# RWKV in a hybrid trunk: the inverse joined to blocks of 64 on TensorE, transitions and states kept per head

## The chip, the cores and the metric

The kernel runs on one core of one Trainium2 chip. The metric is the device time of one execution in microseconds, the median of several runs. Matrix products run on TensorE (PE, with its weight loads as PEld), element-wise work on VectorE (DVE), ScalarE (ACT) and GpSimd (POOL); SyncE (SP) issues most DMAs. Each engine takes its instructions strictly in order.

## What is computed

A two-layer trunk over 512 tokens (256 context, 256 latent) of width 1024. Each layer has four token mixers, and one of them is a bidirectional RWKV-7 with 8 heads of 64. Its recurrence, run once forward and once backward, is all that the change touches:

```python
def _rwkv7_scan(s0, seq, d, reverse):
    def step(s, inp):
        r_t, w_t, k_t, v_t, kk_t, a_t = inp
        s = (s * w_t[:, :, None, :]
             - jnp.einsum('bhvk,bhk->bhv', s, kk_t)[..., None] * (kk_t * a_t)[:, :, None, :]
             + v_t[..., None] * k_t[:, :, None, :])
        return s, jnp.einsum('bhvk,bhk->bhv', s, r_t)
    s_fin, o = lax.scan(step, s0, xs, reverse=reverse)
```

The state `s` is 64x64 per head. Context starts from zero, latent tokens start from the state that the context leaves. In layer 1 only the latent outputs are wanted.

## The kernel before

The sequence is cut into 8 chunks of 64 tokens, and the scan into products of matrices within a chunk and a short recurrence from chunk to chunk. `rwkv()` runs over four pairs of heads `i` (two heads share the 128 partitions) and in each over two directions `d`. For a pair the phases are, in the order of the code: projections of the pair (`pre`, L543 to L568), the decay and the chunk matrices of each direction (`f0`, `f1`, L580 to L697), the inverse (`inv`, L698 to L762), then the projections of the *next* pair, then `b0` (L774 to L822), `b1` (L824 to L862) and the group norm (`fin`, L864 to L882).

**Inverse.** Each chunk has a unit triangular system of 64. `inv` inverts its two diagonal blocks of 32, in `Wt` (drawn as `Wz`): blocks of 16 by substitution on DVE (L730, L732), transposed twice (L739, L740), then joined to 32 by two bursts of 64 products of 16x16x16 (L749 and the like; drawn as `Pr,U` and `Pr,Ai`), and written to `Wt` by ACT (L760) and DVE (L761). The coupling between the two blocks of 32 is not in `Wt`: POOL copies it to `U2` (L721).

**b0** applies the inverse to `B_` per direction and half `q`: four products with `Wt` into a bank, ACT copies the bank to `y1` (L788), 8 products with `U2` (L793, drawn `y,U`), copies to `y2` (DVE L794, ACT L795), 8 more products with the lower block of `Wt` into the first bank (L799, drawn `y,Wz`), and then the copies `Ev` (L801) and `fv` (L804, L805). Then per direction the transitions `GT` of the chunks: identity plus 16 products (L818, drawn `bkt,Ev`), a pair of heads at once as [128, 128], with the products between different heads masked away by a DVE multiplication with `bd` (L821).

**b1** is the recurrence: seven steps `n`, both directions in turn. A step is one product `bkt`·`fv` of 128x128x128, from the second step on one `GT`·`Z` of the same size, and a DVE scaling that writes the next `Z` (L837). The state `Z` is [128, 8, 128], of which only the two diagonal blocks are read. Then come the readouts (drawn `sr,Ev`, `sr,fv`, `re,Z`).

**What sets the order.** All products go through the helper `mm` at L352, so that the profile gives them one line; they are told apart by their operands. Between the phases stand calls of `fill`: they hand out the products of the gate projection (drawn `hh,wh`, `hl,wh`, `hh,wl`, of 512 columns in layer 0 and 256 in layer 1), work that nothing in RWKV waits for and that keeps PE busy. They are called fillers here. A scheduler orders the instructions of each engine from the code, its dependencies and its own costs, so the diff does not show where fillers end up. PSUM has eight banks: 0 and 1 for projections and fillers, 2 and 3 for `inv`, 4 to 6 for `b0`, `b1` and the norm, 7 for the output. One f32 product shows as two records on PE.

Of the kernel before, what the change touches and what calls it, by code (L numbers as in the profile page):

```python
# [9 lines left out]
F32 = mybir.dt.float32  # L10
# [3 lines left out]
AF = mybir.ActivationFunctionType  # L14
OP = mybir.AluOpType
# [279 lines left out]
class Trunk:  # L295
# [210 lines left out]
    def rwkv(self, l, dst, yo):  # L506
        nc, A, tc = self.nc, self.A, self.tc
        last = l == NL - 1
# [8 lines left out]
        with ExitStack() as es:  # L517
# [53 lines left out]
            for i in range(4):  # L571
# [145 lines left out]
                V_.scalar_tensor_tensor(A16, Ai[:, :, 0:16], lo16, Ai[:, :, 16:32], op0=OP.mult, op1=OP.add)  # L717

                U2 = R.tile([128, 2, 8, 32], F32, name="U2")
                for o in (0, 64):  # L720
                    G_.tensor_copy(U2[o:o + 32], U[o:o + 32, :, :, o // 64, 32:64])  # L721
                X2 = Xt[:, 0:512].rearrange("p (t e s) -> p t e s", t=16, e=2)
# [34 lines left out]
                for q in range(4):  # L757
                    sl = slice(32 * q, 32 * q + 32)
                    wt = Wt[sl, :, sl].rearrange("p z (e t) -> p e t z", e=2)
                    nc.scalar.activation(wt[:, 0], xt[sl, :, 0, :], AF.Copy, scale=lo16[sl])  # L760
                    V_.scalar_tensor_tensor(wt[:, 1], xt[sl, :, 1, :], hi16[sl], p2v[sl].rearrange("p z t -> p t z"),  # L761
                                            op0=OP.mult, op1=OP.add)  # L762
                while self.early:
                    self.fill(1)
# [10 lines left out]
                for d in range(2):  # L775
# [4 lines left out]
                    for q in range(2):  # L780
                        py = self.ps("bx")
                        pv = py.rearrange("p (s c) -> p s c", s=4)
                        for s in range(4):
                            self.mm(pv[:, s, :], Wt[:, 8 * d + 4 * q + s, :], B_[:, 4 * q + s, :], start=(s == 0),
                                    stop=False)
                        y12 = R.tile([128, 2, 4, 128], F32, name="y12", tag=("S0" if q == 0 else "S1") if last else "Ai" if q == 0 else "Xi")
                        y1, y2 = y12[:, 0], y12[:, 1]
                        nc.scalar.activation(y1, pv, AF.Copy)  # L788
                        p2 = self.ps("bx")
                        p2v = p2.rearrange("p (s c) -> p s c", s=4)  # L790
                        for s in range(4):
                            for o in (0, 64):
                                self.mm(p2v[o + 32:o + 64, s, :], U2[o:o + 32, d, 4 * q + s, :], y1[o:o + 32, s, :])  # L793
                        V_.tensor_copy(y2[32:64], p2v[32:64])  # L794
                        nc.scalar.activation(y2[96:128], p2v[96:128], AF.Copy)  # L795
                        for s in range(4):
                            for o in (32, 96):
                                sl = slice(o, o + 32)
                                self.mm(pv[sl, s, :], Wt[sl, 8 * d + 4 * q + s, sl], y2[sl, s, :], start=False,  # L799
                                        stop=(s == 3))  # L800
                        nc.scalar.activation(Ev[:, 2 * q:2 * q + 2].rearrange("p c h k -> p (c h) k"),  # L801
# [5 lines left out]
                for d in range(2):  # L807
# [7 lines left out]
                    for c2 in range(4):  # L815
                        for par in range(2):
                            o = 64 * par
                            self.mm(pts[par][:, c2 * 128:c2 * 128 + 128], Ev[o:o + 64, c2],  # L818
                                    bkt[o:o + 64, 2 * c2 + par, :], start=False)
                    for par in range(2):  # L820
                        V_.tensor_mul(GT[:, par:8:2, :], pts[par].rearrange("p (c k) -> p c k", c=4),  # L821
                                      bd[:, None, :].to_broadcast([128, 4, 128]))  # L822
                self.fill(FQ[l][i][3])
                self.phase(f"rw{l}.{i}.b1")  # L824
                orders = ((0, 1, 2, 3, 4, 5, 6, 7), (3, 2, 1, 0, 7, 6, 5, 4))
                for d in range(2):
                    Z = R.tile([128, 8, 128], F32, name="Z", tag="Z" if d else "Z0" if last else "Xi")
                    G_.memset(Z[:, orders[d][0], :], 0.0)
                    ZZ.append(Z)
                for n in range(7):  # L830
                    for d in range(2):
                        Z, c, cn = ZZ[d], orders[d][n], orders[d][n + 1]
                        pz = self.ps("bx")
                        self.mm(pz[:, 0:128], BKT[d][:, c, :], FV[d][:, c], start=True, stop=(n == 0))
                        if n:
                            self.mm(pz[:, 0:128], GG[d][:, c, :], Z[:, c, :], start=False)
                        V_.tensor_scalar(Z[:, cn, :], pz[:, 0:128], PT[d][:, c:c + 1], None, op0=OP.mult)  # L837
                for d in range(2):
# [19 lines left out]
                    for c in range(q0, 8):  # L858
                        for h in range(2):
                            hs = slice(64 * h, 64 * h + 64)  # L860
                            self.mm(po[hs, 64 * c:64 * c + 64], Z[hs, c, hs], re[hs, c - q0, :], start=False,
                                    stop=(d == 1 and c == 7))  # L862
# [1147 lines left out]
```

## Time and profile before

| | us |
|---|---|
| median of 3 runs | 3611.53 (3610.74 to 3620.73) |
| the profiled execution | 3617.56, its span 3615.6 |
| RWKV of layer 0, four pairs | about 160 to 640 of the span |
| RWKV of layer 1, four pairs | about 1716 to 2090 of the span |

Most of the rest of the span (other mixers, the expert layers from about 2580 on) doesn't share code with the change. The mean granted clock of TensorE over the span was 0.942 of full speed; its two levels are 1.2 and 2.4 GHz.

How to read the rows further down: a row of a timeline gives the start in us, the duration in us (of a group of xN instructions, from the first start to the last end), engine, line, operation, `out<-in`, tile and shape, and in brackets the idle time just before with what ended it. Records of PE overlap, so the price of a group is the distance from its start to the next start, not its duration.

### The profile page before, as it was taken

Reading aid. Unit: us, or ns where it says so; the run is one execution under the profiler, and the core shown is the slowest. Engines: PE = TensorE matmul, PEld = TensorE weight load, DVE = VectorE, ACT = ScalarE, POOL = GpSimd, SP = SyncE. Lnnn points to the kernel's source line nnn. Section 1 sums busy time; section 2 is a strip of 40 time slices with the busy share of each in tenths; the row PEclk is TensorE's granted clock in tenths of the full one; section 3 lists DMA queues with packets and bytes.
Section 4 is the critical chain, followed back from the end, with each engine's and each line's share of the span. In section 5 each row is a group of like instructions: output and inputs, shape, how many; then the busy total and the mean of one; then the engine's idle time right before and its main releaser. Section 6 shows DMA issues by size and latency. Waiting matters only on the chain. (4 is left out here: it accounts for less than half of the span.)

```text
span 3615.6 us, 53416 instructions
## 1 busy us (share of the span) xinstructions
PE 3303.8 (91%) x20522; PEld 2560.1 (71%) x20522; DVE 2305.2 (64%) x3375; ACT 1688.3 (47%) x2509; POOL 943.0 (26%) x873
## 2 busy tenths in 40 slices
PE   7999999998878999998988898877899999999998
PEld 3477677776656677776776687666787877877776
DVE  3555653257985423226565536885799889888887
ACT  3333433332333322234443444343677677777675
POOL 2222322134444344444322333544100000000000
PEclk9999999998989999998998899877899999999999
DMA  7511112322115255532111243114599899899895
GB/s 234 163 58 51 59 53 83 112 70 74 54 34 188 83 151 167 158 107 76 57 54 46 67 130 103 51 52 158 220 354 348 341 356 339 323 361 360 332 354 220
DMA packets 195895, 596.82 MB, mean 165 GB/s; under 512 B 22440, under 2 KB 48490, under 8 KB 152112
## 3 DMA queue, kind: packets, MB, share of 16 engines
q1 hardware_dynamic: 177824, 564.15, 44.4%
q10 hardware_dynamic: 17808, 29.18, 2.4%
q8 instruction: 163, 2.67, 0.3%
q14 instruction: 100, 0.82, 0.1%
HBM read 576.53 MB, written 16.71 MB: 164 GB/s over the span
## 5 line engine op out<-in xcount | busy, mean ns | idle before, releaser
L378 DVE TENSOR_TENSOR mwl<-mw,mwh 128x1024 fp32r<-128x1024 f32 x672 | 796.2, 1227 | 43.0 <-ACT mwh L375 41.9
L378 POOL TENSOR_TENSOR wl<-w,wh 128x512 fp32r<-128x512 f32 (+1 forms) x436 | 576.2, 1327 | 914.7 <-ACT wh L375 775.7
L375 ACT ACTIVATE wh<-w 128x512 fp32r<-128x512 f32 x536 | 333.5, 626 | 823.7 <-PE bank L352 580.5
L375 ACT ACTIVATE mwh<-mw 128x1024 fp32r<-128x1024 f32 x672 | 674.9, 1054 | 77.5 <-PE bank L352 73.5
L352 PE MATMUL bank<-mwh,mX 128*128 128x512 f32 x1792 | 570.9, 396 | 0.0
L352 PE MATMUL bank<-hh,wh 128*128 128x512 f32 (+1 forms) x1152 | 438.5, 382 | 31.6 <-ACT hh L481 5.1
L352 PE MATMUL bank<-hh,wl 128*128 128x512 f32 (+1 forms) x1152 | 433.4, 377 | 21.9 <-DVE wl L378 11.6
L352 PE MATMUL bank<-hl,wh 128*128 128x512 f32 (+1 forms) x1152 | 431.0, 374 | 1.8 <-DVE hl L482 1.7
L352 PEld LDWEIGHTS bank<-mwh,mX 128*128 128x128 f32 x1792 | 336.8, 188 | 76.2
L352 PE MATMUL bank<-mwl,mX 128*128 128x512 f32 x896 | 366.7, 409 | 2.2
L352 PEld LDWEIGHTS bank<-hh,wh 128*128 128x128 f32 x1152 | 232.4, 202 | 86.1 <-issue 30.9
L352 PE MATMUL bank<-mwh,mgT 128*128 128x512 f32 x896 | 283.4, 395 | 0.0
L352 PEld LDWEIGHTS bank<-hh,wl 128*128 128x128 f32 x1152 | 231.8, 201 | 65.1 <-DVE wl L378 14.1
L352 PEld LDWEIGHTS bank<-hl,wh 128*128 128x128 f32 x1152 | 232.8, 202 | 48.5 <-issue 16.1
L352 PEld LDWEIGHTS bank<-mwl,mX 128*128 128x128 f32 x896 | 168.4, 188 | 56.5 <-DVE mwl L378 20.9
L352 PEld LDWEIGHTS bank<-mwh,mgT 128*128 128x128 f32 x896 | 168.2, 188 | 40.4
L352 PE MATMUL bank<-mwl,mgT 128*128 128x512 f32 x448 | 178.4, 398 | 0.4
L1724 POOL TENSOR_SCALAR mPg<-moec,rtq,rtG 128x128 f32<-128x128 f32 x16 | 20.9, 1315 | 573.7 <-PE bank L1726 549.7
L378 DVE TENSOR_TENSOR wl<-w,wh 128x512 fp32r<-128x512 f32 x100 | 83.2, 837 | 99.7 <-ACT wh L375 95.3
L352 PE MATMUL bank<-fhh,wl 128*128 128x512 f32 x352 | 137.6, 392 | 1.7 <-POOL wl L378 1.7
L352 PE MATMUL bank<-fhh,wh 128*128 128x512 f32 x352 | 138.7, 397 | 0.0
L352 PE MATMUL bank<-fhl,wh 128*128 128x512 f32 x352 | 137.7, 391 | 0.9 <-DVE fhl L482 0.9
(569 smaller groups left out, 5816.8 us busy)
## 6 DMA issues: line engine op xcount, KB each, us to landing
mw<-in_moe_dram SPq DMA_DIRECT2D x336, 1024.0 KB, 6.3
w<-in_win_dram SPq DMA_DIRECT2D x304, 256.0 KB, 2.8
adaw<-in_ada_dram SPq DMA_DIRECT2D x192, 256.0 KB, 3.8
w<-in_ffn_dram SPq DMA_DIRECT2D x128, 256.0 KB, 3.0
w<-in_wbr_dram SPq DMA_DIRECT2D x64, 256.0 KB, 2.9
gdram<-gth ACTq DMA_DIRECT2D x32, 256.0 KB, 2.0
bth<-gdram SPq DMA_DIRECT2D x32, 256.0 KB, 3.5
w<-in_wout_dram SPq DMA_DIRECT2D x32, 256.0 KB, 5.4
```

Of the source, the lines that this page charges most:

```text
L352: return self.nc.tensor.matmul(out, lhsT, rhs, start=start, stop=stop, skip_group_check=True)
L375: nc.scalar.activation(xh, x, AF.Copy)
L378: (nc.gpsimd if lo == "p" else nc.vector).tensor_tensor(xl, x, xh.bitcast(F32), op=OP.subtract)
L1724: nc.gpsimd.tensor_scalar(Pg, slots[:, 0:CAP], qq[:, t, e:e + 1], G[:, t, e:e + 1], op0=OP.is_equal, op1=OP.mult)
```

## The change

The inverse is completed to blocks of 64 in `inv`: the upper-left inverse is transposed (two DVE transposes), 32 products of 32x32x32 with `U` give T2 (drawn `Pr,U` 32x32), ACT and DVE copy it out of the bank, 32 more products with the lower-right inverse (drawn `Wz,Ai` 32x32) give the missing block, and ACT and DVE copy it into `Wt`. With it `b0` needs a single product per chunk and head; `U2`, `y12`, their 16 products per half and their copies go. `GT` is made of 32 products of 64x64x64 per direction pair in place of 16 of 64x128x128, so that nothing is to be masked, and is copied out by DVE and ACT. The state `Z` shrinks to [128, 8, 64], and each product of the recurrence is split into one per head. `Z` of the first direction has a buffer of its own in both layers.

```diff
-                U2 = R.tile([128, 2, 8, 32], F32, name="U2")
-                for o in (0, 64):
-                    G_.tensor_copy(U2[o:o + 32], U[o:o + 32, :, :, o // 64, 32:64])
...
+                p1, p2 = self.mx_ps(), self.mx_ps()
+                p1v, p2v = [x.rearrange("p (z t) -> p z t", z=16) for x in (p1, p2)]
+                Wn = Pt_[:, 0:512].rearrange("p (z t) -> p z t", z=16)
+                T2 = At[:, 512:1024].rearrange("p (z t) -> p z t", z=16)
+                for o in (0, 64):
+                    sl = slice(o, o + 32)
+                    V_.transpose(Wn[sl], Wt[sl, :, sl])
+                for z in range(16):
+                    for o in (0, 64):
+                        self.mm(p1v[o + 32:o + 64, z], U[o:o + 32, z // 8, z % 8, o // 64, 32:64], Wn[o:o + 32, z])
+                nc.scalar.activation(T2[32:64], p1v[32:64], AF.Copy)
+                V_.tensor_copy(T2[96:128], p1v[96:128])
+                for z in range(16):
+                    for o in (0, 64):
+                        hi = slice(o + 32, o + 64)
+                        self.mm(p2v[o:o + 32, z], T2[hi, z], Wt[hi, z, hi])
+                nc.scalar.activation(Wt[0:32, :, 32:64], p2v[0:32], AF.Copy)
+                V_.tensor_copy(Wt[64:96, :, 96:128], p2v[64:96])
...
-                            self.mm(pv[:, s, :], Wt[:, 8 * d + 4 * q + s, :], B_[:, 4 * q + s, :], start=(s == 0),
-                                    stop=False)
-                        y12 = R.tile([128, 2, 4, 128], F32, name="y12", tag=("S0" if q == 0 else "S1") if last else "Ai" if q == 0 else "Xi")
-                        y1, y2 = y12[:, 0], y12[:, 1]
-                        nc.scalar.activation(y1, pv, AF.Copy)
-                        p2 = self.ps("bx")
-                        p2v = p2.rearrange("p (s c) -> p s c", s=4)
-                        for s in range(4):
-                            for o in (0, 64):
-                                self.mm(p2v[o + 32:o + 64, s, :], U2[o:o + 32, d, 4 * q + s, :], y1[o:o + 32, s, :])
-                        V_.tensor_copy(y2[32:64], p2v[32:64])
-                        nc.scalar.activation(y2[96:128], p2v[96:128], AF.Copy)
-                        for s in range(4):
-                            for o in (32, 96):
-                                sl = slice(o, o + 32)
-                                self.mm(pv[sl, s, :], Wt[sl, 8 * d + 4 * q + s, sl], y2[sl, s, :], start=False,
-                                        stop=(s == 3))
+                            self.mm(pv[:, s, :], Wt[:, 8 * d + 4 * q + s, :], B_[:, 4 * q + s, :])
...
-                        for par in range(2):
-                            o = 64 * par
-                            self.mm(pts[par][:, c2 * 128:c2 * 128 + 128], Ev[o:o + 64, c2],
-                                    bkt[o:o + 64, 2 * c2 + par, :], start=False)
-                    for par in range(2):
-                        V_.tensor_mul(GT[:, par:8:2, :], pts[par].rearrange("p (c k) -> p c k", c=4),
-                                      bd[:, None, :].to_broadcast([128, 4, 128]))
+                        for h in range(2):
+                            hs = slice(64 * h, 64 * h + 64)
+                            for par in range(2):
+                                o = 64 * par
+                                self.mm(pts[par][hs, c2 * 128 + 64 * h:c2 * 128 + 64 * h + 64], Ev[o:o + 64, c2, h],
+                                        bkt[o:o + 64, 2 * c2 + par, hs], start=False)
+                    V_.tensor_copy(GT[:, 0:8:2, :], pts[0].rearrange("p (c k) -> p c k", c=4))
+                    nc.scalar.activation(GT[:, 1:8:2, :], pts[1].rearrange("p (c k) -> p c k", c=4), AF.Copy)
...
-                        self.mm(pz[:, 0:128], BKT[d][:, c, :], FV[d][:, c], start=True, stop=(n == 0))
+                        for h in range(2):
+                            hs = slice(64 * h, 64 * h + 64)
+                            self.mm(pz[hs, 0:64], BKT[d][:, c, hs], FV[d][:, c, h], start=True, stop=(n == 0))
                         if n:
-                            self.mm(pz[:, 0:128], GG[d][:, c, :], Z[:, c, :], start=False)
-                        V_.tensor_scalar(Z[:, cn, :], pz[:, 0:128], PT[d][:, c:c + 1], None, op0=OP.mult)
+                            for h in range(2):
+                                hs = slice(64 * h, 64 * h + 64)
+                                self.mm(pz[hs, 0:64], GG[d][hs, c, hs], Z[hs, c, :], start=False)
+                        V_.tensor_scalar(Z[:, cn, :], pz[:, 0:64], PT[d][:, c:c + 1], None, op0=OP.mult)
```

Where the scheduler puts this on PE is seen at three places. The number after a bank or tile only tells allocations apart.

First, PE in layer 0, pair 1, where the inverse ends and `b0` begins. Before, the products with `Wt` follow on fillers and on the column norm `t,rwc` of the next pair's projections, with the first `y,U` of a half behind four fillers:

```order
751 L352 MATMUL bank2_2615<-t0_2613,rwc_354 128x512
752 L352 MATMUL bank5_2624<-B__2014,Wz_530 128x128 x4
753 L352 MATMUL bank4_2653<-B__2014,Wz_530 128x128 x4
754 L352 MATMUL bank1_2771<-hh_265,wh_2774 128x512
755 L352 MATMUL bank1_2771<-hl_266,wh_2774 128x512
756 L352 MATMUL bank1_2771<-hh_265,wl_2775 128x512
757 L352 MATMUL bank1_2771<-hh_265,wh_2774 128x512
758 L352 MATMUL bank6_2631<-y12_2629,U2_2228 32x128 x8
```

Now the join stands ahead of `t,rwc`, in four pieces among fillers, behind twelve fillers that follow `Pr,Ai`:

```order
732 L352 MATMUL bank0_2669<-hh_265,wh_2672 128x512
733 L352 MATMUL bank2_2432<-Pr_2249,U_1993 32x32
734 L352 MATMUL bank0_2669<-hl_266,wh_2672 128x512
735 L352 MATMUL bank0_2669<-hh_265,wl_2673 128x512
736 L352 MATMUL bank0_2669<-hh_265,wh_2672 128x512
737 L352 MATMUL bank2_2432<-Pr_2249,U_1993 32x32 x31
738 L352 MATMUL bank0_2669<-hl_266,wh_2672 128x512
739 L352 MATMUL bank0_2669<-hh_265,wl_2673 128x512
740 L352 MATMUL bank0_2669<-hh_265,wh_2672 128x512
741 L352 MATMUL bank0_2669<-hl_266,wh_2672 128x512
742 L352 MATMUL bank3_2433<-Wz_530,Ai_2247 32x32
```

Fillers that stood between the pieces of `y` now stand between the pieces of the join; twelve more follow before `t,rwc`, and sixteen between the third and the fourth group of `B_,Wz`.

Second, PE in the recurrence of layer 0, pair 0. Before, single products of the two kinds, with fillers at the beginning:

```order
L352 MATMUL bank_1909<-hh,wh 128x512
L352 MATMUL bank_1715<-Z,GT 128x128
L352 MATMUL bank_1719<-fv,bkt 128x128
L352 MATMUL bank_1719<-Z,GT 128x128
L352 MATMUL bank_1909<-hl,wh 128x512
L352 MATMUL bank_1723<-Z,GT 128x128
L352 MATMUL bank_1727<-fv,bkt 128x128
L352 MATMUL bank_1727<-Z,GT 128x128
L352 MATMUL bank_1731<-fv,bkt 128x128
L352 MATMUL bank_1731<-Z,GT 128x128
```

Now pairs of products, with readouts `sr,fv` between them and no filler:

```order
L352 MATMUL bank_1710<-fv,bkt 64x64 x2
L352 MATMUL bank_1714<-fv,bkt 64x64 x2
L352 MATMUL bank_1718<-fv,bkt 64x64 x2
L352 MATMUL bank_1585<-sr,fv 64x64 x3
L352 MATMUL bank_1718<-Z,GT 64x64 x2
L352 MATMUL bank_1724<-fv,bkt 64x64 x2
L352 MATMUL bank_1724<-Z,GT 64x64 x2
L352 MATMUL bank_1730<-fv,bkt 64x64 x2
L352 MATMUL bank_1585<-sr,fv 64x64 x2
L352 MATMUL bank_1730<-Z,GT 64x64 x2
```

The fillers went elsewhere, and part of the readout came forward into the loop.

Third, PE in layer 1, pair 2, from the products of 16 to the first fillers of `b0`. Before:

```order
L352 MATMUL bank_16265<-twd,rwup 128x512
L352 MATMUL bank_16266<-twd,rwup 128x512
L352 MATMUL bank_15547<-Pr,U 16x16 x64
L352 MATMUL bank_15548<-Pr,Ai 16x16 x64
L352 MATMUL bank_15895<-t_15893,rwc 128x512
L352 MATMUL bank_15904<-B__15297,Wz 128x128 x4
L352 MATMUL bank_15933<-B__15297,Wz 128x128 x4
L352 MATMUL bank_15911<-y_15909,U_15508 32x128 x8
L352 MATMUL bank_15904<-y_15909,Wz 32x128 x8
L352 MATMUL bank_15963<-B__15437,Wz 128x128 x4
L352 MATMUL bank_16373<-hh,wh 128x256
```

Now (the first two `twd,rwup` belong to the next pair):

```order
L352 MATMUL bank_15707<-Pr,Ai 16x16 x64
L352 MATMUL bank_16396<-hh,wl 128x256
L352 MATMUL bank_16454<-twd,rwup 128x512
L352 MATMUL bank_16455<-twd,rwup 128x512
L352 MATMUL bank_15847<-Pr,U 32x32 x32
L352 MATMUL bank_15848<-Wz,Ai 32x32 x32
L352 MATMUL bank_16126<-t_16124,rwc 128x512
L352 MATMUL bank_16135<-B__15459,Wz 128x128 x4
L352 MATMUL bank_16143<-B__15459,Wz 128x128 x4
L352 MATMUL bank_16152<-B__15599,Wz 128x128 x4
L352 MATMUL bank_16133<-sr,fv 64x64 x2
L352 MATMUL bank_16160<-B__15599,Wz 128x128 x4
```

Here the two halves of the join stand next to each other with nothing between. Counted over layer 1, the fillers between the first product of 16 and the output copy `O` go from 117, 69, 69 and 79 in the four pairs to 86, 50, 34 and 32; between `O` and the next pair's first product of 16 there are 7, 35 and 32 more than before, and 58 more behind the last `O`. In layer 0 these counts stay the same, but for 8 fillers that move behind the last `O`.

## Rows read from the trace of the kernel before

**Rows 1.** The page: busy time of each engine, share of the span, instructions.

```profile
PE 3303.8 (91%) x20522; PEld 2560.1 (71%) x20522; DVE 2305.2 (64%) x3375; ACT 1688.3 (47%) x2509; POOL 943.0 (26%) x873
```

**Rows 2.** Busy time by stretch: window, length, engines, PEclk (granted clock), DMA share, GB/s.

```profile
180.00:640.00 460.00, 433.59 (x3947) 327.38 (x3946) 232.33 (x408) 174.48 (x294) 129.82 (x119) 0.96 0.19 62
1640.00:2090.00 450.00, 389.56 (x4093) 319.68 (x4094) 255.51 (x483) 190.41 (x338) 138.01 (x134) 0.90 0.18 59
...
367.67:424.57 56.90, 48.84 (x282) 34.81 (x281) 44.88 (x82) 25.69 (x42) 20.01 (x17) 0.95 0.21 69
```

**Rows 3.** Waits of PE in layer 0, 180:640: total us, times, longest.

```profile
PE bank L352 <- DVE Pr L740: 16.6, 3, 5.6
```

**Rows 4.** Waits of PE in layer 1, 1715:2090, the same columns.

```profile
PE bank L352 <- DVE Pr L740: 18.4, 3, 9.4
PE bank L352 <- issue: 6.3, 5, 2.5
```

**Rows 5.** Timeline of PE in `b0` of layer 0, pair 0.

```profile
195.94 1.06 PE L352 MATMUL bank<-y,U 32*32 32x128 f32 x16
196.93 0.50 PE L352 MATMUL bank<-hl,wh 128*128 128x512 f32 x1
197.27 0.40 PE L352 MATMUL bank<-hh,wl 128*128 128x512 f32 x1
197.50 0.39 PE L352 MATMUL bank<-hh,wh 128*128 128x512 f32 x1
...
201.01 0.40 PE L352 MATMUL bank<-y,Wz 32*32 32x128 f32 x2
201.34 0.50 PE L352 MATMUL bank<-hh,wh 128*128 128x512 f32 x1
...
202.00 1.06 PE L352 MATMUL bank<-y,Wz 32*32 32x128 f32 x14
202.99 1.16 PE L352 MATMUL bank<-B__903,Wz 128*128 128x128 f32 x8
...
204.31 0.34 PE L352 MATMUL bank<-sr,fv 128*64 128x64 f32 x4
204.57 0.50 PE L352 MATMUL bank<-hh,wh 128*128 128x512 f32 x1
```

**Rows 6.** Timeline of PE, same pair: transitions, recurrence, readout.

```profile
217.12 1.16 PE L352 MATMUL bank<-bkt,Ev 64*128 64x128 f32 x8
218.20 0.51 PE L352 MATMUL bank<-hh,wl 128*128 128x512 f32 x1
...
231.05 0.39 PE L352 MATMUL bank<-fv,bkt 128*128 128x128 f32 x2
...
231.50 0.39 PE L352 MATMUL bank<-fv,bkt 128*128 128x128 f32 x2
...
234.39 1.22 PE L352 MATMUL bank<-sr,Ev 64*64 64x64 f32 x48
235.53 0.50 PE L352 MATMUL bank<-hh,wl 128*128 128x512 f32 x1
```

**Rows 7.** Timeline of PE, same pair: the products of 16 in the inverse.

```profile
160.99 1.24 PE L352 MATMUL bank<-Pr,U 16*16 16x16 f32 x128
162.16 1.03 PE L352 MATMUL bank<-adaw,csilu 128*2 128x512 f32 x4
```

**Rows 8.** DVE by line, 100:640: count, busy us, mean ns, idle before it, releasers.

```profile
L837 DVE TENSOR_SCALAR Z<-bank,Pt 128x128 f32<-128x128 f32 x56 | 19.6, 351 | 8.5 <-PE bank L352 3.4
...
L716 DVE STREAM_TRANSPOSE Ai<-U 32x512 f32<-32x512 f32 x16 | 17.2, 1073 | 0.2
...
L566 DVE RECIPROCAL t<-t 128x512 f32<-128x512 f32 x4 | 13.4, 3353 | 0.1
...
L794 DVE COPY y<-bank 32x512 f32<-32x512 f32 x16 | 10.9, 683 | 23.1 <-PE bank L352 23.0
...
L761 DVE SCALAR_TENSOR_TENSOR Wz<-Pr,rwc,bank 32x256 f32<-32x256 f32 x16 | 10.5, 658 | 12.7 <-PE bank L352 12.5
```

More of the change, by code (lines that the diff above doesn't have):

```diff
@@ L826, in rwkv @@
                 for d in range(2):
-                    Z = R.tile([128, 8, 128], F32, name="Z", tag="Z" if d else "Z0" if last else "Xi")
+                    Z = R.tile([128, 8, 64], F32, name="Z", tag="Z" if d else "Z0")
                     G_.memset(Z[:, orders[d][0], :], 0.0)
@@ L860, in rwkv @@
                             hs = slice(64 * h, 64 * h + 64)
-                            self.mm(po[hs, 64 * c:64 * c + 64], Z[hs, c, hs], re[hs, c - q0, :], start=False,
+                            self.mm(po[hs, 64 * c:64 * c + 64], Z[hs, c, :], re[hs, c - q0, :], start=False,
                                     stop=(d == 1 and c == 7))
```

## The prediction

> **What bounds the kernel now.** I read the page's busy times first: PE is busy 91% of the span [rows 1], the next engine, DVE, 64%. An average over stages says little, so I went on to the two stretches that the change touches. In layer 0 PE is busy 433.6 of 460 us at a mean clock of 0.96, in layer 1 389.6 of 450 us at 0.90 [rows 2]. So in layer 0 PE's own work sets the time: its one large wait is for the transpose L740, 16.6 us in three places [rows 3], at the end of the substitution on DVE. It lies between the output `O` of one pair and the inverse of the next; that stretch (56.9 us in one pair, PE busy 48.8 of it) holds DVE for 44.9 us [rows 2], and the change leaves it as it is. From the first product of 16 to `O`, PE stands almost dense, and since the number of fillers there does not change in layer 0, a microsecond of PE work that goes there is a microsecond of time. In layer 1 PE waits more: 18.4 us for L740 in three places, and 6.3 us in which nothing that the profile shows holds it ("issue"), up to 2.5 us at a time [rows 4].
>
> A price of PE is read here as the distance from one start to the next. A filler between fillers takes 0.23 us (197.27 to 197.50), the one that follows a burst of small tiles 0.34 (196.93 to 197.27) [rows 5]: changing the shape costs about 0.11 us.
>
> **The change, part by part** (per pair of heads, at full clock).
>
> *The second half of the solve goes.* For a half of one direction, `y,U` takes 0.99 us (195.94 to 196.93), `y,Wz` 0.33 + 0.99 (201.01 to 201.34, 202.00 to 202.99) [rows 5], and the three interruptions of the fillers 0.11 each: 2.6 us, four times, **-10.4 us**. The copies that go with it (L794, 0.68 us each [rows 8], and ACT's) were hidden under fillers in layer 0.
>
> *Transitions.* Eight records of `bkt,Ev` take 1.08 us behind an identity (217.12 to 218.20) [rows 6]; the 32 records of a pair come in five pieces, about 4.1 us. Now 64 records of 64 columns; the nearest row is `sr,Ev`, 48 of the same tile in 1.14 us (234.39 to 235.53) [rows 6], 24 ns each, so 1.5 us, and 1.0 for the shape changes between the banks: 2.5 us, **-1.6 us**. The masks become copies of the same size, half of them on ACT: no term.
>
> *Recurrence.* One `fv,bkt` and one `Z,GT` take 0.45 us (231.05 to 231.50) [rows 6], 0.225 each, 14 + 12 of them 5.9 us. Now each is two products of 64 columns. Unbroken, four such records would take 4 x 24 ns = 0.10 us; a group of four of 64 columns that stands alone between others took 0.26 (204.31 to 204.57) [rows 5]. The groups of the loop alternate in tile and bank, so they are nearest to the latter: 26 x 0.26 = 6.8 us, **+0.9 us**, with 2.6 us as the other end. Five fillers leave the loop and interrupt it no more: **-0.5 us**. The chain of data per step and direction, product, scaling (0.35 us for 128 columns [rows 8], less for 64), product, stays below the four groups of PE in a step, 1.04 us.
>
> *The join.* 128 records. The bounds are 128 records of 16 columns in 1.17 us (160.99 to 162.16) [rows 7] and the 62 ns of `y,U` with 128 columns on the same 32x32 tile [rows 5], 7.9 us. With 32 columns it should be a little over the first: 2.2 us, and four entries into and out of fillers, twelve shape changes in all, 1.3: **+3.5 us**. Its chain is longer than its work: after L761, two transposes of 32x512 (1.07 each by L716), the first products 0.6, two copies (0.68 by L794, one after the other 1.4), products 0.6, copies 1.4 [rows 8]: 6.1 us. In layer 0 twelve fillers stand ahead of it, four in its middle and twelve behind, and cover it. In layer 1, pairs 1 to 3, the halves stand together and PE waits: 6.1 - 3.5 = 2.6, and a bit of L761 (four of 0.66 us [rows 8]) that `t,rwc` used to cover: **+3 us in each of three pairs**.
>
> *The copies of `fv`.* In pairs 0 to 2 the reciprocal of the next pair (3.35 us [rows 8]) now stands on DVE just ahead of or between these copies, and the fourth group of `B_,Wz` needs the bank that the first copy frees. Sixteen fillers, 3.7 us, stand before it. It can cost nothing or the 3.35 us; I take **+0.5 us**.
>
> *Fillers of layer 1.* 7 + 35 + 32 fillers of 256 columns move out of the dense part into the stretch in which PE waits for L740 anyway (18.4 us [rows 4]). At half of a filler of 512, 0.12 us, that is 8.9 us; some will find no wait: **-5 us** once. The 58 behind the last `O` are only moved. POOL loses `U2`, which nobody waited for, and no DMA is touched.
>
> The sum: a pair -10.4 - 1.6 + 0.9 - 0.5 + 3.5 + 0.5 = -7.6 us, the last pair of a layer, with no reciprocal, -8.1. Layer 0: 3 x -7.6 - 8.1 = -30.9. Layer 1: -7.6 + 2 x (-7.6 + 3) + (-8.1 + 3) - 5 = -26.9. Together -57.8 us. The profiled execution took 3617.56 us, 6 above the median; from it 3559.8, from the median of 3611.53 us **3554 us**.
>
> **The rivals.**
>
> *The chain of the join shows everywhere.* If fillers cover neither L761 nor the chain, each pair pays 2.6 + 6.1 in place of 3.5, +5.2; in eight pairs 42, of which 9 are already in the sum, so +33, and with the 5 of the fillers gone +38: -20, **3592 us**. For it: PE already waits for DVE in layer 1. Against it: in layer 0 28 fillers, 6.4 us, stand around it, and more if the clock is low there.
>
> *A shape change costs the whole length of a record.* A single record of 64 columns lasts about 0.27 us (the group of four lasts 0.34 [rows 5], with starts 24 ns apart as in `sr,Ev` [rows 6]); records of one shape overlap. If each group of the recurrence had to end before the next begins, 26 groups would take 0.10 + 0.27 each, 9.7 us in place of 6.8, +2.9 a pair, +23 in all: -35, **3577 us**. The Trainium skill, "TensorEngine Tiling (Array Packing)", section Tiling Modes, speaks for it: changing the tiling mode drains the engine. This trace agrees only with a small price for that, the 0.11 us at a filler behind small tiles.
>
> *Slower: PE starves for instructions.* The change puts 84 more records a pair on PE, almost all of 32 to 64 columns. The "issue" waits of up to 2.5 us [rows 4] came in the runs of 256 records of 16 columns. If each of five new dense places (two halves of the join, two transitions, the recurrence) paid one such wait, that would be 12.5 us a pair, 100 in all: +42, **3654 us**. It decides from 7.2 us a pair, three such waits. Against it: the 48 records of `sr,Ev` ran through at 24 ns with no such wait [rows 6].
>
> *The change does not do what it says.* Only if the scheduler gave the time back elsewhere; the counts of fillers speak against it.
>
> **How the numbers follow.** The forecast 0.66, the chain everywhere 0.14, the drain 0.10, starvation 0.06, something else 0.04. The forecast's own bounds: below, the join at 1.2 us a half, the recurrence at part of its 2.6 us and no wait in layer 1, some -30; above, the join towards 7.9, +35, which is the same as the first rival. So **3522 to 3594 us**, which leaves out starvation and the worst of the first rival. A measurement of this kernel can tell 0.3% from no change, 10.8 us. The forecast, the drain and most of the first rival lie beyond it: faster 0.86, within it 0.07, slower 0.07.
>
> **What would show it.** In the profile after, from the first product of 16 to `O` in layer 0 should be 7 to 8 us shorter in each pair, and the stretch from `O` to the next inverse still about 57. 128 records of 32x32x32 should take 2 to 3.5 us in all; if they take 8, the join's term was wrong. The seven steps of the recurrence should take some 7 us; at 10 the drain is right, at 3 the split is nearly free. A wait for the copies or for the transposes of the join in layer 0 would show the first rival, "issue" beside the new products the third. It would also be wrong if the clock fell to its lower level in the recurrence, where PE now runs small tiles alone, without fillers.

## The result and the profile after

| | before | changed |
|---|---|---|
| median, us | 3613.16 | 3535.58 (3527.66 to 3537.91) |
| ratio, 95% interval | | 0.978 [0.9766, 0.9794] |
| span of the profiled execution, us | 3615.6 | 3532.2 |

The change saves 77.6 us, 2.1%. The forecast was 3554 us, a saving of 57.8: the direction and the range held, the size was a quarter too small. As the experiments show, the share put down to the join was far too small, and the one put down to the states was a loss of 3 us where they cost some 11.

The page of the changed kernel, first part (busy time, share, instructions), answers to [rows 1]: the same shares of a shorter span, with 672 records more on PE.

```profile
PE 3229.6 (91%) x21194; PEld 2504.9 (71%) x21194; DVE 2284.4 (65%) x3359; ACT 1667.2 (47%) x2477; POOL 930.7 (26%) x857
```

The windows that answer to [rows 2]: layer 0, layer 1, and the stretch from `O` to the next inverse (length, busy time of PE, PEld, DVE, ACT, POOL, granted clock, DMA share, GB/s):

```profile
180.00:610.00 430.00, 401.54 (x4209) 306.78 (x4208) 218.30 (x398) 166.43 (x282) 132.54 (x114) 0.95 0.22 71
1640.00:2020.00 380.00, 332.27 (x4331) 272.55 (x4331) 222.48 (x450) 165.13 (x299) 120.93 (x122) 0.90 0.21 65
...
346.02:402.91 56.89, 48.80 (x283) 34.62 (x281) 44.90 (x82) 25.58 (x42) 18.95 (x16) 0.96 0.21 69
```

The clock of both layers is nearly what it was (0.95 after 0.96, 0.90 in both). The stretch behind `O` (from here on `O` stands for the first product that reads the output copy), 56.90 us before, is 56.89 now. So what was saved in layer 0 was saved between the first product of 16 and `O`: 66.85 and 66.26 us in pairs 1 and 2 became 57.52 and 56.73. From the first pair's inverse in layer 0 to the first in layer 1 the trace has 1514.9 us in place of 1555.0 (-40.0); from there to the last `O` 323.5 in place of 371.1 (-47.6, of which the 58 moved fillers, some 7 us, come back behind it).

Waits of PE in layer 0, 180:610 (total us, times, longest), against [rows 3]. The wait for the substitution is the same; new is mainly the wait for the copy of `fv`. None of the join's copies or transposes is in the list. The window begins behind the join of pair 0; there PE waits for none of them in this trace, and 0.5 us for a transpose in the second trace of the same kernel, below.

```profile
PE bank L352 <- DVE Pr L736: 16.7, 3, 5.6
...
PE bank L352 <- DVE fv L804: 1.4, 3, 0.5
```

Waits of PE in layer 1, 1640:2020, against [rows 4]. L766 are the transposes of the join, L770 and L771 its first copies.

```profile
PE bank L352 <- DVE Pr L736: 6.0, 2, 5.5
...
PE bank L641 <- DVE BK L623: 5.2, 3, 1.8
PE bank L352 <- ACT wh L375: 5.2, 1, 5.2
...
PE bank L352 <- DVE Pr L766: 3.1, 4, 1.8
PE bank L352 <- DVE fv L804: 2.3, 3, 1.2
PE bank L352 <- ACT Ai L770: 2.0, 3, 0.7
PE bank L352 <- issue: 1.8, 3, 0.9
PE bank L352 <- DVE Ai L771: 1.3, 3, 0.5
```

PE in layer 0, pair 2: the first half of the join. Two records, three fillers, 62 records; the first half costs 0.17 + 1.13 us (412.69 to 412.86, 413.75 to 414.88).

```profile
412.69 0.24 PE L352 MATMUL bank<-Pr,U 32*32 32x32 f32 x2
412.86 0.50 PE L352 MATMUL bank<-hl,wh 128*128 128x512 f32 x1
...
413.75 1.19 PE L352 MATMUL bank<-Pr,U 32*32 32x32 f32 x62
414.88 0.50 PE L352 MATMUL bank<-hl,wh 128*128 128x512 f32 x1
```

The same pair, transitions and recurrence. Thirty records of the transitions take 0.61 us (431.77 to 432.38); a group of four in the recurrence takes 0.26 (437.29 to 437.55, 437.55 to 437.81), as forecast from [rows 5], but the first twelve `fv,bkt` run on in 0.40 (436.30 to 436.70).

```profile
431.77 0.69 PE L352 MATMUL bank<-bkt,Ev 64*64 64x64 f32 x30
432.38 0.51 PE L352 MATMUL bank<-ident 128*128 128x512 f32 x1
...
436.30 0.57 PE L352 MATMUL bank<-fv,bkt 128*64 128x64 f32 x12
436.70 0.40 PE L352 MATMUL bank<-sr,fv 128*64 128x64 f32 x6
437.02 0.33 PE L352 MATMUL bank<-Z,GT 64*64 64x64 f32 x4
437.29 0.34 PE L352 MATMUL bank<-fv,bkt 128*64 128x64 f32 x4
437.55 0.33 PE L352 MATMUL bank<-Z,GT 64*64 64x64 f32 x4
437.81 0.34 PE L352 MATMUL bank<-fv,bkt 128*64 128x64 f32 x4
```

### The profile page after: what moved, and what is told of

Read it like the earlier page. It is cut to its first block, busy times and chain, and to the rows that moved or that the text cites. A ratio compares the mean times of both kernels' runs of the same rounds, so it can differ in the third digit from the quotient of the medians.

```text
span 3532.2 us, 54671 instructions
## 1 busy us (share of the span) xinstructions
PE 3229.6 (91%) x21194; PEld 2504.9 (71%) x21194; DVE 2284.4 (65%) x3359; ACT 1667.2 (47%) x2477; POOL 930.7 (26%) x857
## 3 DMA queue, kind: packets, MB, share of 16 engines
q1 hardware_dynamic: 177824, 564.15, 45.2%
```

## The experiments

The theory was the prediction's: in the dense part TensorE's own work sets the time, and each part of the change is worth its slots there. First the parts one by one, on one chip.

**The changed kernel as a yardstick.**

> The changed kernel once more, as the yardstick for the three runs beside it on the same chip. It should come out near 3535 us, 0.978 to 0.980 of the kernel before, with the same trace: 128 products of 32x32x32 a pair in about 2.6 us of TensorE in layer 0, transitions 2.1 us, the recurrence 5.7 us.

Measured: 3534.27 us, 0.9789 [0.9774, 0.9803]. The experiments from the filler edit on ran on two other chips, each with the kernel before beside it; where they are set against this yardstick, the ratios count more than the microseconds.

**The join alone.** In the changed kernel, transitions and recurrence as before:

```diff
-                        for h in range(2):
-                            hs = slice(64 * h, 64 * h + 64)
-                            for par in range(2):
...
+                        for par in range(2):
+                            o = 64 * par
+                            self.mm(pts[par][:, c2 * 128:c2 * 128 + 128], Ev[o:o + 64, c2],
+                                    bkt[o:o + 64, 2 * c2 + par, :], start=False)
...
-                    Z = R.tile([128, 8, 64], F32, name="Z", tag="Z" if d else "Z0")
+                    Z = R.tile([128, 8, 128], F32, name="Z", tag="Z" if d else "Z0" if last else "Xi")
```

> The join to 64 and the single product in b0 alone; transitions and states as before, with mask and 128x128 products. Theory (TensorE's work sets the time, and each part is worth its own slots): y goes, 9.2 us a pair in layer 0 and 1.3 us of interrupted fillers; the join costs 2.6 there and 3.5 in layer 1 plus about 2 us of waits in three pairs; some -8 us in each of eight pairs less a little, in all -55 to -62, so 3551 to 3558 us (0.983 to 0.985). Rival (the parts help each other, because the scheduler can only close the gaps when GT and Z are small too): clearly less than 0.75 of the whole gain, above 3560 us.

Measured: 3539.56 us, 0.979 [0.9775, 0.9805]: -74 us. Nearly the whole gain is in this part, by the ratios all of it (0.979 and 0.9789); the expectation was 12 to 19 us too modest, and the rival falls clearly.

**Transitions and states per head alone.** In the kernel before, the diff's hunks from `GT` on and nothing of the inverse.

> Transitions and states per head alone; the inverse stays at blocks of 32 with y, U2 and its copies. Theory: transitions -2 us a pair, recurrence 0 to -0.2, a few interruptions of fillers less: -16 to -20 us in all, 3593 to 3597 us (0.9945 to 0.9955), and with the join-only run it adds up to the whole gain of 77 within 5 us. Rival (splitting a product in two costs a drain of the array at each change of shape): no gain or a loss, 3610 us or more.

Measured: 3607.46 us, 0.9989 [0.998, 0.9998]: -6 us, a third of what was expected. The two parts still add up (-74 and -6 against -79). The trace shows what eats the gain of the transitions. Here the scheduler left fillers in the recurrence and the readout behind it (12 in most pairs of layer 0, 14 to 15 in layer 1, against 6 and 10 before), and in layer 0 half of them stand alone between small tiles. A timeline of PE in layer 0, pair 1 of this kernel:

```profile
353.56 0.34 PE L352 MATMUL bank<-fv,bkt 128*64 128x64 f32 x4
353.83 0.50 PE L352 MATMUL bank<-hh,wh 128*128 128x512 f32 x1
354.26 0.33 PE L352 MATMUL bank<-Z,GT 64*64 64x64 f32 x4
```

The filler takes 0.43 us (353.83 to 354.26) where it takes 0.23 among its like [rows 5]: 0.2 us for each such visit. Summed over layer 0 (distances from start to start), the transitions fall by 6.4 us, but the recurrence rises by 2.2 and the fillers by 6.9, of which only 2.1 are for the nine that came in.

**Whole products in the recurrence.** The changed kernel with only `Z` put back:

```diff
-                        for h in range(2):
-                            hs = slice(64 * h, 64 * h + 64)
-                            self.mm(pz[hs, 0:64], BKT[d][:, c, hs], FV[d][:, c, h], start=True, stop=(n == 0))
+                        self.mm(pz[:, 0:128], BKT[d][:, c, :], FV[d][:, c], start=True, stop=(n == 0))
...
-                                self.mm(pz[hs, 0:64], GG[d][hs, c, hs], Z[hs, c, :], start=False)
+                            self.mm(pz[:, 0:128], GG[d][:, c, :], Z[:, c, :], start=False)
```

> The changed kernel with only the recurrence put back to whole products of 128x128x128 and a state of [128, 8, 128]; join and per-head transitions stay. Theory: a group of two products of 64 columns takes 0.26 us, as much as one of 128 columns with its neighbours (0.23), so that this split is worth nothing: within 4 us of the changed kernel beside it. Rival 1 (the split was the part that gained, by 1 us a pair or more): 8 us slower or more. Rival 2 (the changes of shape cost): 8 us faster or more.

Measured: 3522.93 us, 0.9733 [0.9714, 0.9752], 11 us faster than the changed kernel beside it (3534.27), and the intervals of the two ratios don't meet. So the theory falls here, and rival 2 is the nearest: the split of the recurrence costs. In steps: join alone 3539.6, with the transitions per head 3522.9 (-17), with the states per head 3534.3 (+11). Where the 11 us go is not all to be seen. In layer 0, from the first inverse to the last `O`, the traces are alike (398.8 us split, 397.8 whole). In layer 1 the whole products save 6.1 us from the first inverse to the last `O` (326.3 against 320.2). The rest of that one pair of executions lies in stretches that the edit doesn't touch. The first trace of the split kernel has 395.4 and 323.5 us for the two layers, so that two executions of one kernel differ by about 3 us in each, and the place of the 11 us is not shown. The mean clock is not behind it: at 0.943 to 0.944, three executions with whole products took 3522.9 to 3523.2 us, two with the split beside them 3532.3 and 3534.3.

PE's idle time over layer 1 is the same in both, 45.3 us split and 45.2 whole: with whole products the waits at the join shrink, but those with no visible cause are 7.2 us again. One thing that differs is the clock at the join. In both traces of the split kernel the joins of pairs 2 and 3 of layer 1 stand at the lower clock, with whole products mostly at the higher one. Pair 2 (stretch, length, PE busy, granted clock, DMA share, GB/s; split above, whole below):

```profile
1879.90:1885.70 5.80, 4.34 (x128) 0.50 0.04 14
```

```profile
1875.02:1879.47 4.45, 3.28 (x130) 0.81 0.19 63
```

In pairs 1 to 3 the join's products take 3.5, 4.3 and 4.3 us of PE with the split and 2.6, 3.3 and 3.0 with whole products: that is 3.3 of the 6.1 us.

**More fillers at the join of layer 1.** With the split, the order has 19 and 1 fillers ahead of the join in pairs 1 and 2 of layer 1 and 21 in the recurrence; with whole products 29 and 9 at the join and 12 in the recurrence. There are two readings of this, so the filler was moved in both kernels:

```diff
-FQ = (((1, 0, 2, 1, 2, 0),) * 4, ((1, 0, 2, 1, 1, 0),) * 4)
+FQ = (((1, 0, 2, 1, 2, 0),) * 4, ((1, 0, 3, 0, 1, 0),) * 4)
```

> The changed kernel with one filler group of layer 1 called right behind the inverse in place of behind the transitions; nothing else differs. In pairs 1 and 2 of layer 1 the fillers between the last product of 16 and the products with Wt go from 19 and 1 to 35 and 13; inside the recurrence they stay 21. It tells two readings of the 11 us apart that whole 128x128 products in the recurrence saved. Theory A (the split recurrence draws fillers away from the join, and TensorE waits there): 4 to 8 us faster than the changed kernel, 3527 to 3531 us, and the waits for the join's copies and transposes in these pairs shrink. Theory B (fillers between small tiles inside the recurrence cost it, 21 against 12): within 3 us of the changed kernel, 3532 to 3538.

> The same filler edit on the kernel with whole 128x128 products in the recurrence (join and per-head transitions kept): 38 and 29 fillers at the join of pairs 1 and 2 of layer 1, 12 inside the recurrence. Theory A: its join was covered in pair 1 already, so 0 to 4 us more than the 3523 us without the edit: 3518 to 3523. Theory B: no change, 3520 to 3525. It should be the fastest so far or as fast.

Measured: 3529.65 us, 0.977 [0.9756, 0.9784] for the split; 3522.43 us, 0.9763 [0.974, 0.9786] for whole products, where nothing is gained against 3522.93. The split kernel goes the way of theory A, by 4.6 us, though its interval meets that of the yardstick, so that the gain isn't shown. The waits of PE at the join in layer 1 (1640:2020, split with the edit) shrink from 6.4 to 4.5 us:

```profile
PE bank L352 <- DVE Pr L766: 2.2, 2, 1.8
PE bank L352 <- ACT Ai L770: 1.4, 2, 0.7
...
PE bank L352 <- DVE Ai L771: 0.9, 2, 0.5
```

With more cover at the join in both, whole products lead by 7 us in the medians, but the two intervals overlap almost wholly (the six times of the last version spread over 27 us). So it isn't shown that a lead is left, and the two theories aren't told apart: fillers drawn from the join and lone fillers between small tiles may both have part in the 11 us.

**One product for both heads.** `GT` is block-diagonal, so that a single product of the full array does both heads with a state of 64 columns:

```diff
-                            for h in range(2):
-                                hs = slice(64 * h, 64 * h + 64)
-                                self.mm(pz[hs, 0:64], GG[d][hs, c, hs], Z[hs, c, :], start=False)
+                            self.mm(pz[:, 0:64], GG[d][:, c, :], Z[:, c, :], start=False)
```

> The changed kernel with GT times Z of both heads as one product of 128x128 by 64 columns (GT is block-diagonal, so one product does both heads); bkt times fv stays split. If the number and the tile of the products cost (two of 64x64, a shape of their own): the 96 products become 48 on the tile of the fillers, 0.05 to 0.1 us a group less, 2 to 8 us faster than the changed kernel. If only the change from one group to the next costs, whatever its tile: within 2 us, and the layer-0 slots of these products stay at 2.9 us a pair.

Measured: 3542.8 us, 0.9809 [0.9793, 0.9826], 8 us *slower* than the changed kernel's 3534.27, which neither side expected. The intervals of the two ratios touch (0.9793 and 0.9803), but the trace says the same: in layer 0 the slots of `Z,GT` rise from 11.5 to 17.3 us, 4.3 a pair where 2.9 or less was expected. The timeline of PE in layer 0, pair 2, of this kernel, and under it of the one with whole products:

```profile
443.62 0.34 PE L352 MATMUL bank<-fv,bkt 128*64 128x64 f32 x4
443.88 0.43 PE L352 MATMUL bank<-Z,GT 128*128 128x64 f32 x2
444.25 0.34 PE L352 MATMUL bank<-fv,bkt 128*64 128x64 f32 x4
```

```profile
441.25 0.33 PE L352 MATMUL bank<-sr,fv 128*64 128x64 f32 x2
441.51 0.49 PE L352 MATMUL bank<-Z,GT 128*128 128x128 f32 x2
441.83 0.39 PE L352 MATMUL bank<-fv,bkt 128*128 128x128 f32 x2
...
442.76 0.39 PE L352 MATMUL bank<-fv,bkt 128*128 128x128 f32 x2
442.99 0.39 PE L352 MATMUL bank<-Z,GT 128*128 128x128 f32 x2
443.21 0.39 PE L352 MATMUL bank<-fv,bkt 128*128 128x128 f32 x2
```

Two records of 64 columns on the full array take 0.37 us behind a tile of 128x64 (443.88 to 444.25), two of 128 columns among their like 0.22 (442.99 to 443.21), and behind a tile of 128x64 0.32 (441.51 to 441.83). Half the columns, and dearer: what makes the difference is the change of tile, about 0.10 us on the way into the full array, and the one product has a change on the way out as well. It depends on which tiles change: a group of four that alternates between 128x64 and 64x64 takes 0.26 us, where four of 128x64 that run on into a readout of the same tile take 0.17 and four of 64x64 in a long run 0.10, so that a change costs some 0.10 to 0.16 there.

**A longer chain at the join.** Each of its four copies twice:

```diff
                 nc.scalar.activation(T2[32:64], p1v[32:64], AF.Copy)
                 V_.tensor_copy(T2[96:128], p1v[96:128])
+                nc.scalar.activation(T2[32:64], p1v[32:64], AF.Copy)
+                V_.tensor_copy(T2[96:128], p1v[96:128])
...
                 nc.scalar.activation(Wt[0:32, :, 32:64], p2v[0:32], AF.Copy)
                 V_.tensor_copy(Wt[64:96, :, 96:128], p2v[64:96])
+                nc.scalar.activation(Wt[0:32, :, 32:64], p2v[0:32], AF.Copy)
+                V_.tensor_copy(Wt[64:96, :, 96:128], p2v[64:96])
```

> The changed kernel with each of the four copies of the join made twice (the same data written again), which makes the chain from the join's first product to the new block in Wt about 2.6 us longer (0.6 on ScalarE and 0.7 on VectorE, twice). Theory: in layer 0 fillers cover the chain, so nothing changes there; in layer 1, pairs 1 to 3, TensorE waits for it already, so it grows by 2 to 2.6 us in each, 6 to 8 us in all: 3541 to 3544 us. Rival (the chain stands on the path in all eight pairs): +17 to +21 us, 3553 to 3557 us.

Measured: 3544.16 us, 0.9816 [0.98, 0.9831], 9.9 us more than the yardstick; the intervals of the ratios just touch. Waits of PE in layer 0 (180:610):

```profile
PE bank L352 <- DVE Pr L736: 16.7, 3, 5.6
...
PE bank L352 <- DVE fv L808: 0.9, 3, 0.5
```

and in layer 1 (1640:2020), where L781, L772 and L773 are copies of the join:

```profile
PE bank L352 <- DVE Wz L781: 12.6, 3, 6.0
...
PE bank L352 <- ACT Ai L772: 4.0, 3, 2.0
...
PE bank L352 <- DVE Ai L773: 1.4, 3, 0.5
```

In layer 0 no new wait for the join appears (ahead of the window, in pair 0, PE waits 0.5 us for a transpose, as in the yardstick), and the four stretches from the inverse to `O` add up to 225.6 us against 224.9: there the chain is covered. In layer 1 the waits for the join grow from 6.4 to 17.9 us, but not evenly: from 1.1 and 2.0 to 7.4 and 6.8 in pairs 1 and 2, while in pair 3 they fall from 3.3 to 2.5 and pair 0 now waits 1.3. The scheduler moved fillers here too: 22 stand ahead of the join in each of pairs 1 to 3 in place of 19, 1 and 7, and in pairs 1 to 3 of layer 0 eight more stand around it. So the total came out as the theory had it, 9.9 us with 6 to 8 expected, but not its split by pairs, and the run doesn't price the chain of a pair. The first rival of the prediction (the chain on the path in all eight pairs) falls; in the changed kernel what it names is real in three pairs of eight.

**Products of `bkt` and `fv` ahead of the recurrence**, and **the identity added on VectorE**:

```diff
+                pzs = [self.ps("bx") for _ in range(2)]
+                for d in range(2):
+                    for n in range(7):
...
+                            self.mm(pzs[d][hs, 64 * n:64 * n + 64], BKT[d][:, c, hs], FV[d][:, c, h], start=(n == 0),
+                                    stop=(n == 0))
```

```diff
-                    for pt in pts:
-                        self.mm(pt.rearrange("p (c k) -> p c k", c=4), self.identr,
-                                self.identr[:, None, :].to_broadcast([128, 4, 128]), start=True, stop=False)
...
+                        V_.tensor_add(GT[:, par:8:2, :], pts[par][:, 0:256].rearrange("p (c k) -> p c k", c=4),
+                                      i64[:, None, :].to_broadcast([128, 4, 64]))
```

> The changed kernel with the fourteen bkt-fv products of both directions made ahead of the recurrence, into one bank for each direction (seven slots of 64 columns); in the steps only the GT-Z products are added to them. Theory (what costs in the recurrence is the change of shape, about 0.1 us a group, not the columns): 56 records run on at 24 ns, 1.4 us in place of 2.8, and readouts and fillers stand in the gaps of the steps: -1 to -1.5 us a pair, -8 to -12 in all, 3523 to 3528 us. Rival (with the bkt-fv products gone the steps are bound by the chain product, scaling, product of 0.8 us): TensorE waits in the recurrence and the time stays within 4 us of 3535.

> The changed kernel with the identity of the transitions added by VectorE when it copies them out ([128, 8, 64], 256 columns a bank), so that the four products of 128x512 with the identity go. Theory: 4 x 0.40 us of TensorE a pair, -1.6 in each of eight, -13 in all: 3521 to 3524 us. Rival (TensorE then waits for VectorE's adds, which were split between two engines): within 4 us of 3535.

> The two edits together: bkt-fv products ahead of the recurrence, and the identity added on VectorE. If TensorE's own work sets the time in the dense part, they add up: -21 to -25 us, 3510 to 3515 us. If each only moves the wait to VectorE's chain, the second adds nothing to the first: above 3520 us.

Measured: 3530.12 us (0.9771 [0.9756, 0.9786]), 3533.39 us (0.9773 [0.9757, 0.9789]), and both together 3521.67 us (0.974 [0.9727, 0.9754]). Neither edit alone is clear of the yardstick, both together are 13 us faster than it where 21 to 25 were expected. The time lies above 3520 us, where the rival had it, though the second edit did add to the first (3530.1 to 3521.7). In the first, the slots of the recurrence in layer 0 shrink by 8.1 us (distances from start to start in the trace, summed over `fv,bkt` and `Z,GT` of four pairs), but the readouts `sr,Ev` and `re,Z` that now stand in the gaps of the steps get 4.3 us longer; why is not shown, since they have the same tile of 64x64 as `Z,GT`. In the second, the 16 identity products of each layer vanish (6.6 and 6.5 us), but in layer 0 of the profiled execution PE worked 59.5 us at the lower clock in place of 42.5, and the four stretches from the inverse to `O` came out 3 us longer.

**A trial of several together**, with one `GT`-`Z` product and off-diagonal blocks zeroed on GpSimd:

```diff
+                    G_.memset(GT, 0.0)
...
+                            V_.tensor_add(GT[hs, par:8:2, hs], pts[par][hs, 0:256].rearrange("p (c k) -> p c k", c=4),
+                                          self.ident[hs, None, hs].to_broadcast([64, 4, 64]))
...
+                            self.mm(pz, GG[d][:, c, :], Z[:, c, :], start=False)
```

> A trial for a faster version: the changed kernel with bkt-fv products ahead of the recurrence, one GT-Z product for both heads, the identity of the transitions added on VectorE (off-diagonal blocks zeroed on GpSimd) and the filler edit. If the parts add up (both first edits gave 3522 us together): 3510 to 3518 us. If TensorE then waits for VectorE's chain in the recurrence and for the added copies: 3520 to 3528 us.

Measured: 3531.71 us, 0.9781 [0.9767, 0.9796]: no better than the changed kernel, and above both ranges. The trace points at the one product on the full array: in layer 0 the slots of `Z,GT` take 16.6 us, against 7.6 in the version with the two edits together. No run has this version without that product, so the rest of the difference stays open. The fastest versions are the one with whole products in the recurrence (3522.9, and 3522.4 with the filler edit) and the one with the two edits together (3521.7), each some 0.3% below the changed kernel; the two can't be combined as they are, since whole products ahead of the recurrence need four banks where there are three.

## Why the prediction was right, and where it was wrong

*What bounds it* held: PE's own work in layer 0, with the stretch behind `O` unchanged at 56.9 us. The signs that it named were there: the 128 records of the join took 2.6 us, and from the first `fv,bkt` to the last `Z,GT` it was 7.2 us in pairs 0 to 2 of layer 0 (9.0 in pair 3, where more readouts stand between), not the 10 of the drain.

*Term by term in layer 0.* From the distances between starts, summed by operation over four pairs of the traces of before and after, and divided by four:

| term, us a pair | forecast | measured |
|---|---|---|
| `y,U` and `y,Wz` gone, with fewer interrupted fillers | -10.4 - 0.5 | -9.2 - 1.9 |
| transitions | -1.6 | -2.0 (4.1 to 2.1) |
| recurrence | +0.9 | -0.2 (5.9 to 5.7) |
| join | +3.5 | +2.6 |
| wait for `fv` | +0.5 | +0.3 |
| sum | -7.6 | -10.4 |

The first row was right within 0.2 us. The others were each too pessimistic by 0.2 to 1.1. For the join I took 2.2 us plus twelve shape changes; it ran at 18 ns a record with a few changes, 1.3 us a half. For the transitions I took a full microsecond of shape changes between banks where the 64 records, changes and all, took 2.1. For the recurrence 26 groups of 0.26 were counted; the price of one was right, but the first twelve records came in one go, and in front of readouts of the same tile a group took only 0.17 (the readouts' own slots grew by 0.2 us a pair). In four pairs these terms come to some 10 us more than forecast; layer 0 beat its forecast by 9 (-40.0 against -30.9).

*Layer 1* beat it by 14 us (-40.6 net of the moved fillers, against -26.9), and here a step failed. It isn't PE's own work: `y`, transitions, recurrence and join come to -32.6 us where the sum had -30.4. That the join took the forecast 3.5 us a pair here is luck: two of the four ran at the lower clock and took 4.3 us, the others 2.6 and 2.7. It is the waits: the sum charged PE with the new ones at the join (9 us forecast, 6.4 measured) and didn't take off those that go with `y`. They stood in the same view of the kernel before, 1715:2090:

```profile
PE bank L352 <- DVE y L794: 1.6, 2, 0.8
PE bank L352 <- DVE Wz L761: 1.5, 2, 0.7
PE bank L352 <- ACT y L795: 1.1, 2, 0.9
```

4.2 us, gone after. The waits with no visible cause, 6.3 us [rows 4], became 1.8: the prediction held them for a threat to new dense runs, and they shrank (in the version with whole products they are 7.2 again, so this may not be owed to the change). The moved fillers did what was forecast and more: the wait for L740 of 18.4 us [rows 4] is 6.0 now, though other waits in the same stretches (L623, and ACT's `wh`) took some of it. In the three stretches from `O` to the next inverse PE's idle time fell from 32.2 to 23.7 us, 8.5 where 5 were forecast. In all PE's idle time in layer 1 fell by 8 us, where the sum had it rise by about 6, and that makes up nearly all of the 14 us.

*The split by parts* was wrong in a way that the total hides. Of the 57.8 us some 13 were put down to transitions, less than nothing to the recurrence, and 48 to the join and `y`, the waits and the moved fillers. Measured in steps it is -74 for the join, -17 for the transitions, +11 for the states. The step that failed for the last is the recurrence's term, which priced the groups of the loop by themselves. By themselves they came out right (their slots in layer 0 are 22.9 us split, 25.4 whole). It left out what fillers cost between them, 0.43 against 0.23 us in the run with heads alone, and what happens where the scheduler fetches them from: the join of layer 1 at the lower clock. How the 11 us divide stays open.

*The rivals.* The chain shows in three pairs of eight, as the sum had it, and not in layer 0 (doubled copies: no new wait there). Starvation for instructions didn't appear: the waits with no visible cause shrank. The price of a change of tile is neither 0.11 us everywhere nor a whole record. The Trainium skill, "TensorEngine Tiling (Array Packing)", section Tiling Modes, says that a change of tiling mode drains the engine. The runs agree that it costs, from some 0.10 us into the full array and 0.10 to 0.16 between 128x64 and 64x64 to 0.2 around a lone filler. The split of the recurrence did cost, +11 us against the +23 of the rival, but how much of that is changes of tile is not shown; the change as a whole gained.

## What to carry to other kernels

A step that is made once, in a few dense runs of small products at a place with cover (the join), was worth far more here than the same work spread over every chunk with copies between: look for work that can be moved from the many uses of a matrix into the matrix itself. When summing a change, list the waits that go away as carefully as those that come; they stand in the same view. And price a small product by the tiles of its neighbours, fillers above all: a product of half the columns can be dearer than the whole one if it changes the tile.

## What was not expected of the hardware

Two records of 64 columns on the full array behind a 128x64 tile took 0.37 us, two of 128 columns among their like 0.22 and behind that tile 0.32. A filler of 512 columns alone between 64-column tiles took 0.43 in place of 0.23. Records of 32x32x32 ran at 18 ns each, those of 16x16x16 at 9 [rows 7], those of 64x64x64 at 20 to 24. What part of the 11 us of the split recurrence lies in layer 1's order and what in the clock of stretches that no edit touches stays open: one pair of executions showed 6 us in layer 1, and between the layers PE worked 80.7 us at the lower clock with the split and 72.2 with whole products, in a stretch that came out 4.5 us shorter, although their mean clock over the whole span was the same (0.944).
